# A two-layer hybrid encoder on one Trainium2 core: the recurrent projection is copied to SBUF before its convolution taps

## The chip, the core and the metric

The kernel runs on one core of one Trainium2 chip. The metric is the device time of one execution in microseconds (us). Before the change it is 1476.55 us, the median of three runs (1475.07, 1476.55, 1477.28).

## The reference, cut to what matters

The program computes two residual layers and a final RMS norm over 1024 positions with 1024 channels. The even layer is Fourier mixing beside grouped attention. The change is in the odd layer, a recurrent block of width 2048:

```python
h = rms_norm(x, norm_g)
xr, gate = jnp.split(h @ w_in, 2, axis=-1)            # 2048 recurrent and 2048 gate channels
xp = jnp.pad(xr, ((0, 0), (CONV_LEFT, CONV_WIDTH - 1 - CONV_LEFT), (0, 0)))
xc = conv_b + xp[:, 0:s] * conv_w[0]                  # depthwise, 4 taps at -2, -1, 0, +1
for j in range(1, CONV_WIDTH):
    xc = xc + xp[:, j:j + s] * conv_w[j]
y = (rglru_scan(xc, w_a[0], b_a[0], w_x[0], b_x[0], lam[0], reverse=False)
     + rglru_scan(xc, w_a[1], b_a[1], w_x[1], b_x[1], lam[1], reverse=True))
return x + (y.astype(x.dtype) * jax.nn.silu(gate)) @ w_out
```

`rglru_scan` takes two sigmoid gates of `xc` per direction (block-diagonal matrices of 128x128 over 16 blocks), forms decays from them and runs a linear recurrence along the positions.

## The kernel before, in words

Channels lie on the 128 partitions and positions along the free axis, so a tile `M` is 128x1024 float32 and holds one block of 128 channels. TensorE (PE) multiplies float32 values that are split into a high and a low part: every product is three matmuls (`mm3`, L222 to L224: high by high, high by low, low by high), 128x512 each. A projection of one block is 8 input blocks by 2 halves of the positions by 3, so 48 matmuls. Its result is a PSUM tile `pa` of 128x1024, of which there are three (`A`, L154). A weight arrives by DMA in one of 3 tiles `W`; ACT copies it to a high part `Wh` (L180, the rows CAST Wh<-W), and DVE subtracts that for the low part `Wl` (L181). There are 4 `Wh` and 4 `Wl` tiles, so a CAST Wh waits until PE has read an earlier weight for the last time.

The odd layer (`odd`, L1084) handles its 16 blocks in 16 steps j, which the table `SCHED` (L19) describes. In a step

- **the gate groups**: `gates` (L1112) makes four PSUM tiles, one for each direction and kind of gate, called gate groups 1 to 4 here. Each is 6 matmuls on the split rows of block j, and is emptied by one sigmoid on ACT (L1122);
- **G**: the letter G in `SCHED` is a projection of a gate block, 48 matmuls, emptied by a SiLU on ACT (L1164). In steps 1 to 5 one G lies among the gate groups;
- **P**: the letter P is a recurrent projection, 48 matmuls, followed by `conv` (L1098). In steps 0 to 5 one P lies beside the scans, so step j makes the row of block j+2;
- **the scans**: `scans` (L1125) runs tanh, exp and square root on ACT (L1129 to L1134) and products and two recurrences on DVE (L1128 to L1148).

Later steps hold pieces F of the output projection (`out_part`, L794), whose input is read back from DRAM and split by CAST M<-Q on ACT and a subtraction on DVE. The first eight of those casts stand between steps 5 and 6.

In `conv`, ACT makes the centre tap with the bias straight from PSUM (L1101), and DVE adds the other three taps, also from PSUM (L1105, three instructions), then makes the high part (L1108) and the low part (L1109) that the gate groups multiply. The PSUM tile is free for another product when the third tap has read it.

Instructions are not placed by hand alone. Each engine runs its own queue in order; a scheduling layer (Tile) orders the instructions of each queue from the data they need, from priorities (`self.first(n)`, L188, moves a piece ahead) and from its own estimate of costs. Adding an instruction can therefore move others, on the same engine and on other ones.

Of the kernel before, what the change touches and what calls it, by code (L numbers as in the profile page):

```python
# [137 lines left out]
class Trunk:  # L138
# [945 lines left out]
    def odd(self):  # L1084
        nc, a, par = self.nc, self.a, self.par
# [11 lines left out]

        def conv(j, ps):  # L1098
            with self.first(200):
                xc, xr = self.S(), ps  # L1100
                nc.scalar.activation(xc, ps, AF.Identity, bias=col("cb", j), scale=col("cw", 32 + j))  # L1101
                for tap, o in ((0, -2), (1, -1), (3, 1)):
                    d = slice(max(0, -o), 1024 - max(0, o))
                    s = slice(max(0, o), 1024 + min(0, o))
                    nc.vector.scalar_tensor_tensor(xc[:, d], xr[:, s], col("cw", tap * 16 + j), xc[:, d],  # L1105
                                                   op0=ALU.mult, op1=ALU.add)
                h, low = self.S(F32R), self.S(F32R)
                nc.vector.tensor_copy(h, xc)  # L1108
                nc.vector.tensor_sub(low, xc, h)  # L1109
                return xc, (h, low)  # L1110
# [81 lines left out]
        def item(c):  # L1192
            n = made[c]
            made[c] += 1
            if c == "P":
                return steps(n, lambda ps: rows.__setitem__(n, conv(n, ps)))
            return steps(16 + n, lambda ps: sgs.__setitem__(n, gate_path(n, ps)))
# [8 lines left out]
        for c, (ps, w) in zip(FIRST, start):  # L1206
            self.gemm(ps[:, HALF[1]], w, self.h, HALF[1])
            n = made[c]
            made[c] += 1
            if c == "P":  # L1210
                rows[n] = conv(n, ps)
            else:
                sgs[n] = gate_path(n, ps)
        for _ in items(BEFORE):
            pass
        for j, (kinds, then, chunks) in enumerate(SCHED):
            xc, xhl = rows.pop(j)
# [56 lines left out]
```

## Time and profile before

| | |
|---|---|
| median of the runs | 1476.55 us |
| the profiled execution's own time | 1476.9 us |
| its span, first to last instruction | 1475.1 us |
| PE busy | 1434.8 us (97%) |
| DVE busy | 1177.0 us (80%) |
| ACT busy | 855.7 us (58%) |
| mean granted clock of PE | 0.989 |

All durations below are of this one execution. A row of the profile names the line of the kernel, the engine, the operation and its tiles (`out<-in`, buffer numbers left out). In the timeline the first two numbers are the start and the length in us, and a bracket at the end gives how long the engine had been idle before the instruction and what it waited for. A time there counts from the first instruction of the span. A granted clock of 1.00 is full speed.

### The profile page before, as it was taken

The numbers are of one execution on the slowest core, as the hardware profiler recorded it, in microseconds if no ns is written. First come the engines' busy times: TensorE is split into PE (matmuls) and PEld (weight loads), VectorE is DVE, ScalarE is ACT, GpSimd is POOL, SyncE is SP. The second block draws the span as 40 slices with busy tenths as digits, with TensorE's granted clock in tenths as the row PEclk, the third lists the DMA queues.
The fourth block names the chain that finished last, engine by engine and source line by source line (L and its number), as shares of the span: only waits on it lengthen the run. The fifth ranks groups of instructions, "written<-read, shape, count | busy, mean of one in ns | idle before, by whom it ended". The sixth has DMA issues, their size and how long they took to land.

```text
span 1475.1 us, 17430 instructions
## 1 busy us (share of the span) xinstructions
PE 1434.8 (97%) x6468; PEld 1176.1 (80%) x6468; DVE 1177.0 (80%) x1459; ACT 855.7 (58%) x983; POOL 95.1 (6%) x182
## 2 busy tenths in 40 slices
PE   8999999999998999999999999998999999999997
PEld 6897888888696888788888878777788888887787
DVE  8768979889638787887857768988897989789574
ACT  7635435434326877878734365776658567667143
POOL 0210101000000000000000000000000000001000
PEclk9999999999988999999999999999999999999999
DMA  7733435456655345534456312231413434235552
GB/s 272 268 120 110 172 115 191 171 194 249 243 203 182 129 165 214 179 143 157 144 190 211 127 51 64 72 107 53 147 65 107 129 129 157 79 117 197 168 203 100
DMA packets 79706, 224.67 MB, mean 152 GB/s; under 512 B 9794, under 2 KB 12100, under 8 KB 79620
## 3 DMA queue, kind: packets, MB, share of 16 engines
q1 hardware_dynamic: 60148, 159.40, 33.0%
q0 software_dynamic: 17808, 62.04, 10.7%
q10 hardware_dynamic: 1664, 2.10, 0.4%
q8 instruction: 51, 0.84, 0.2%
q14 instruction: 35, 0.29, 0.1%
HBM read 152.04 MB, written 66.22 MB: 148 GB/s over the span
## 4 chain that ended last, share of the span: by engine, by line
PE 59%; issue 33%; DVE 3%; ACT 2%; POOL 1%; DMA 1%; SPq 0%; POOLq 0%; DVEq 0%; ACTq 0%
PE pa L222 16%; PE pa L223 16%; PE pa L224 15%; PE pb L222 3%; PE pb L223 3%; PE pb L224 2%; PE pb L843 2%; POOL x2d L174 1%; ACT M L180 1%; PE pa L436 1%; PE pb L869 1%; POOL yd L174 1%; DVE M L181 0%; DMA M<-x1d 0%; ACT Wh L180 0%
## 5 line engine op out<-in xcount | busy, mean ns | idle before, releaser
L222 PE MATMUL pa<-M,Wh 128*128 128x512 f32 (+1 forms) x1328 | 514.2, 388 | 17.4 <-ACT M L340 5.5
L223 PE MATMUL pa<-M,Wh 128*128 128x512 f32 (+1 forms) x1328 | 513.4, 387 | 0.2 <-DVE M L181 0.2
L224 PE MATMUL pa<-M,Wl 128*128 128x512 f32 (+1 forms) x1328 | 510.9, 385 | 0.0
L222 PEld LDWEIGHTS pa<-M,Wh 128*128 128x128 f32 x1328 | 250.3, 188 | 74.9 <-ACT M L1122 8.1
L223 PEld LDWEIGHTS pa<-M,Wh 128*128 128x128 f32 x1328 | 250.3, 188 | 52.7 <-DVE M L181 1.8
L224 PEld LDWEIGHTS pa<-M,Wl 128*128 128x128 f32 x1328 | 250.3, 188 | 50.5 <-issue 0.7
L180 ACT CAST Wh<-W 128x1024 fp32r<-128x1024 f32 (+1 forms) x120 | 118.3, 989 | 273.1 <-PE pa L223 190.1
L181 DVE TENSOR_TENSOR Wl<-W,Wh 128x1024 fp32r<-128x1024 f32 (+1 forms) x120 | 137.2, 1147 | 50.4 <-ACT Wh L180 50.3
L180 ACT CAST M<-M 128x1024 fp32r<-128x1024 f32 (+3 forms) x134 | 112.1, 854 | 77.4 <-DVE M L444 35.9
L222 PE MATMUL pa<-M,M 128*128 128x512 f32 (+1 forms) x368 | 144.8, 394 | 10.0 <-DVE M L779 3.4
L181 DVE TENSOR_TENSOR M<-M,M 128x1024 fp32r<-128x1024 f32 (+3 forms) x134 | 128.9, 976 | 28.0 <-ACT M L180 27.2
L223 PE MATMUL pa<-M,M 128*128 128x512 f32 (+1 forms) x368 | 143.2, 389 | 0.2 <-DVE M L181 0.2
L224 PE MATMUL pa<-M,M 128*128 128x512 f32 (+1 forms) x368 | 142.8, 388 | 0.0
L223 PE MATMUL pb<-M,Wh 128*128 128x512 f32 x272 | 106.4, 391 | 2.2 <-DVE M L181 2.2
L222 PE MATMUL pb<-M,Wh 128*128 128x512 f32 x272 | 106.4, 391 | 0.2 <-DVE Q L825 0.2
L224 PE MATMUL pb<-M,Wl 128*128 128x512 f32 x272 | 106.1, 390 | 0.0
L845 DVE TENSOR_REDUCE mx<-pb 128x1 f32<-128x512 f32 x128 | 85.1, 681 | 21.8 <-PE pb L843 21.5
L1122 ACT ACTIVATE M<-pa,par 128x1024 f32<-128x1024 f32 x64 | 70.4, 1116 | 54.2 <-PE pa L224 49.7
L222 PEld LDWEIGHTS pa<-M,M 128*128 128x128 f32 x368 | 71.6, 195 | 26.9 <-ACT M L180 3.3
L904 ACT ACTIVATE M<-pa 128x1024 f32<-128x1024 f32 x64 | 65.7, 1027 | 44.0 <-PE pa L224 43.6
L181 DVE TENSOR_TENSOR M<-Q,M 128x512 fp32r<-128x512 f32 x120 | 77.4, 685 | 11.5 <-ACT M L180 11.4
L180 ACT CAST M<-Q 128x512 fp32r<-128x512 f32 x120 | 69.7, 617 | 28.9 <-DMA Q<-yd 9.7
(221 smaller groups left out, 1926.9 us busy)
## 6 DMA issues: line engine op xcount, KB each, us to landing
W<-wo SPq DMA_DIRECT2D x32, 512.0 KB, 3.7
W<-w SPq DMA_DIRECT2D x32, 512.0 KB, 3.6
W<-wa SPq DMA_DIRECT2D x22, 512.0 KB, 4.5
qd<-M POOLq DMA_DIRECT2D x16, 512.0 KB, 4.0
M<-hd SPq DMA_DIRECT2D x16, 512.0 KB, 4.5
M<-wf SPq DMA_DIRECT2D x16, 512.0 KB, 5.6
M<-qd SPq DMA_DIRECT2D x16, 512.0 KB, 5.7
x1d<-Q POOLq DMA_DIRECT2D x32, 256.0 KB, 2.3
```

Source lines behind the costliest of these rows:

```text
L174: self.nc.gpsimd.dma_start(out=dst, in_=src)
L180: self.nc.scalar.copy(h, src)
L181: self.nc.vector.tensor_sub(l, src, h)
L222: mm(out, w[0], x[0], start=start, stop=False, **k)
L223: mm(out, w[0], x[1], start=False, stop=False, **k)
L224: mm(out, w[1], x[0], start=False, stop=stop, **k)
L436: nc.tensor.matmul(s[:, q], self.onesr, sq.at(q)[l], start=l == 0, stop=l == 1)
L843: nc.tensor.matmul(ps, qh[:, t * 128:t * 128 + 128], self.kh[hd // 4][:, HALF[u]], start=True, stop=True)
L845: nc.vector.reduce_max(mx[:, 2 * t + u:2 * t + u + 1], ps, axis=mybir.AxisListType.X)
L869: nc.tensor.matmul(s, self.onesr, acc[l][:, q], start=l == 0, stop=l == 1)
L904: nc.scalar.activation(e, ps, AF.Exp, scale=SCALE)
L1122: nc.scalar.activation(s, ps, AF.Sigmoid, bias=col("gb", (2 * j + d) * 2 + i))
```

## The change

Two lines of `conv` change. ACT first copies the projection from PSUM to a new tile `xr` in SBUF, and the three taps read that copy. The centre tap still reads PSUM. Everything behind it moves by one line number (L1105 becomes L1106, and so on).

```diff
         def conv(j, ps):
             with self.first(200):
-                xc, xr = self.S(), ps
+                xc, xr = self.S(), self.S()
+                nc.scalar.copy(xr, ps)
                 nc.scalar.activation(xc, ps, AF.Identity, bias=col("cb", j), scale=col("cw", 32 + j))
                 for tap, o in ((0, -2), (1, -1), (3, 1)):
                     d = slice(max(0, -o), 1024 - max(0, o))
                     s = slice(max(0, o), 1024 + min(0, o))
                     nc.vector.scalar_tensor_tensor(xc[:, d], xr[:, s], col("cw", tap * 16 + j), xc[:, d],
                                                    op0=ALU.mult, op1=ALU.add)
```

There are 16 such copies, one for each block, and the scheduling layer orders the queues anew. Three places matter for what follows.

First ACT's queue in step 3, before the change, from the convolution's centre tap on. `pa_7625` is the recurrent projection, `pa_7702`, `pa_7730`, `pa_7751` and `pa_7772` are gate groups 1 to 4, and `Wh_7809` is a weight's high part:

```order
L1101 ACTIVATE M_7684<-pa_7625,par_63 128x1024
L1122 ACT_TABLE_LOAD
L1122 ACTIVATE M_7709<-pa_7702,par_63 128x1024
L1122 ACTIVATE M_7737<-pa_7730,par_63 128x1024
L180 CAST Wh_7809<-W_7711 128x1024
L1122 ACTIVATE M_7758<-pa_7751,par_63 128x1024
L1122 ACTIVATE M_7779<-pa_7772,par_63 128x1024
L1164 ACT_TABLE_LOAD
L1164 ACTIVATE M_7793<-pa_7717 128x1024
L180 CAST Wh_7886<-W_7807 128x1024
```

The same place now, with the copy. `pa_7633` is the projection, `pa_7712`, `pa_7740`, `pa_7761` and `pa_7782` are the gate groups, and `Wh_7819` is the weight that was `Wh_7809`:

```order
L1101 COPY M_7693<-pa_7633 128x1024
L1102 ACTIVATE M_7692<-pa_7633,par_63 128x1024
L180 CAST Wh_7819<-W_7721 128x1024
L1123 ACT_TABLE_LOAD
L1123 ACTIVATE M_7719<-pa_7712,par_63 128x1024
L1123 ACTIVATE M_7747<-pa_7740,par_63 128x1024
L1123 ACTIVATE M_7768<-pa_7761,par_63 128x1024
L180 CAST Wh_7898<-W_7817 128x1024
L1123 ACTIVATE M_7789<-pa_7782,par_63 128x1024
L1165 ACT_TABLE_LOAD
L1165 ACTIVATE M_7803<-pa_7727 128x1024
```

The CAST of the weight stood behind the sigmoids of gate groups 1 and 2 and stands ahead of them now; in both programs it waits for the same instruction of PE, the last but one matmul of step 3's projection G (its last reader is a high-by-low product). The following CAST came up from behind the SiLU to ahead of the fourth sigmoid. Steps 2 and 4 are changed in the same way; in step 5 the CAST (of a 128x512 weight there) stands between the centre tap and the sigmoids in both programs.

Next PE's queue in the same step before the change, around gate group 2 (`pa_7730`), which stands inside the projection G (`pa_7717`) with 40 of its 48 matmuls ahead of it:

```order
L224 MATMUL pa_7717<-M_7017,Wl_7622 128x512
L222 MATMUL pa_7717<-M_7053,Wh_7621 128x512
L222 MATMUL pa_7730<-M_7501,Wh_7525 128x512
L223 MATMUL pa_7730<-M_7502,Wh_7525 128x512
L224 MATMUL pa_7730<-M_7501,Wl_7526 128x512
L222 MATMUL pa_7730<-M_7501,Wh_7525 128x512
L223 MATMUL pa_7730<-M_7502,Wh_7525 128x512
L224 MATMUL pa_7730<-M_7501,Wl_7526 128x512
L223 MATMUL pa_7717<-M_7053,Wh_7621 128x512
```

And now, gate group 2 being `pa_7740` and G `pa_7727`, with 16 of the 48 ahead of it:

```order
L224 MATMUL pa_7727<-M_6785,Wl_7630 128x512
L222 MATMUL pa_7727<-M_6790,Wh_7629 128x512
L222 MATMUL pa_7740<-M_7509,Wh_7533 128x512
L223 MATMUL pa_7740<-M_7510,Wh_7533 128x512
L224 MATMUL pa_7740<-M_7509,Wl_7534 128x512
L222 MATMUL pa_7740<-M_7509,Wh_7533 128x512
L223 MATMUL pa_7740<-M_7510,Wh_7533 128x512
L224 MATMUL pa_7740<-M_7509,Wl_7534 128x512
L223 MATMUL pa_7727<-M_6790,Wh_7629 128x512
```

Gate group 2 moved 24 matmuls towards the start of G. It takes the PSUM tile that the convolution gives back: before, its first matmul waits for the third tap on DVE; now for the centre tap on ACT. Gate groups 3 and 4 still follow the end of G, and each waits for a sigmoid: group 3 for that of group 1, group 4 for that of group 2.

Last, ACT's queue ahead of step 6 before the change, from a centre tap (of `pa_8189`) on: six casts of the output projection's input stand ahead of the weight's CAST and two behind it.

```order
L1101 ACTIVATE M_8248<-pa_8189,par_63 128x1024
L180 CAST M_8262<-Q_8260 128x512
L180 CAST M_8267<-Q_8265 128x512
L180 CAST M_8272<-Q_8270 128x512
L180 CAST M_8277<-Q_8275 128x512
L180 CAST M_8282<-Q_8280 128x512
L180 CAST M_8287<-Q_8285 128x512
L180 CAST Wh_8340<-W_8323 128x1024
L180 CAST M_8292<-Q_8290 128x512
L180 CAST M_8297<-Q_8295 128x512
L1122 ACT_TABLE_LOAD
```

The same place now:

```order
L1101 COPY M_8263<-pa_8203 128x1024
L1102 ACTIVATE M_8262<-pa_8203,par_63 128x1024
L180 CAST Wh_8356<-W_8339 128x1024
L180 CAST M_8278<-Q_8276 128x512
L180 CAST M_8283<-Q_8281 128x512
L180 CAST M_8288<-Q_8286 128x512
L180 CAST M_8293<-Q_8291 128x512
L180 CAST M_8298<-Q_8296 128x512
L180 CAST M_8303<-Q_8301 128x512
L180 CAST M_8308<-Q_8306 128x512
L180 CAST M_8313<-Q_8311 128x512
```

The weight's CAST is ahead of all eight. It waits for PE to reach the end of that step's G in both programs. From step 7 on PE's queue keeps its order, and ACT's gains the copies and moves a few casts.

## The prediction

> **What bounds the kernel now.** I read the page first, then the busy time in stretches of 30 us, PE's waits, and the timeline around those waits.
>
> ```profile
> span 1475.1 us, 17430 instructions
> PE 1434.8 (97%) x6468; PEld 1176.1 (80%) x6468; DVE 1177.0 (80%) x1459; ACT 855.7 (58%) x983; POOL 95.1 (6%) x182
> 1090.00:1120.00 30.00, 30.00 (x134) 24.82 (x133) 25.95 (x23) 15.92 (x16) 1.08 (x2) 1.00 0.29 98
> ```
>
> PE is busy for 97%, and from 1090 to 1330 us, most of the odd layer, it never pauses: 134 matmuls in 30 us, two of them cut by the ends, so 0.226 us each. There, relief of DVE or load on ACT is worth nothing. The change can only act where PE waits, in steps 0 to 6, about 850 to 1062 us. PE's waits there (waiter, waited for, us, times, longest), with one row of the timeline:
>
> ```profile
> PE pa L222 <- DVE M L1105: 4.5, 6, 1.0
> PE pa L222 <- ACT M L1122: 3.7, 2, 2.9
> 865.10 0.47 PE L222 MATMUL pa<-M,Wh 128*128 128x512 f32 x1 [0.24 <-DVE M L1105]
> ```
>
> L1105 is the third tap: PE waits for the PSUM tile that it holds. Step 3 in the timeline:
>
> ```profile
> 947.43 0.39 PE L222 MATMUL pa<-M,Wh 128*128 128x512 f32 x1
> 948.85 0.47 PE L222 MATMUL pa<-M,Wh 128*128 128x512 f32 x1 [1.02 <-DVE M L1105]
> 947.42 1.27 DVE L1105 SCALAR_TENSOR_TENSOR M<-pa,par,M 128x1023 f32<-128x1023 f32 x1
> 940.14 1.19 ACT L1101 ACTIVATE M<-pa,par 128x1024 f32<-128x1024 f32 x1
> 941.34 1.28 ACT L1122 ACT_TABLE_LOAD   x1
> 942.64 1.12 ACT L1122 ACTIVATE M<-pa,par 128x1024 f32<-128x1024 f32 x1
> 950.50 1.12 ACT L1122 ACTIVATE M<-pa,par 128x1024 f32<-128x1024 f32 x1 [6.74 <-PE pa L224]
> 952.08 1.05 ACT L180 CAST Wh<-W 128x1024 fp32r<-128x1024 f32 x1 [0.47 <-PE pa L223]
> ```
>
> The third tap ends at 948.69 and gate group 2 starts 0.16 later. Note the last row: the weight's CAST finds its tile free only at 952.08, when G ends; by then two sigmoids are out of the way. In step 5 it stands ahead of them already:
>
> ```profile
> 997.87 1.18 ACT L1101 ACTIVATE M<-pa,par 128x1024 f32<-128x1024 f32 x1
> 1009.27 0.62 ACT L180 CAST Wh<-W 128x512 fp32r<-128x512 f32 x1 [10.21 <-PE pa L223]
> 1009.91 1.28 ACT L1122 ACT_TABLE_LOAD   x1
> 1011.20 2.12 ACT L1122 ACTIVATE M<-pa,par 128x1024 f32<-128x1024 f32 x2
> 1014.31 1.11 ACT L1122 ACTIVATE M<-pa,par 128x1024 f32<-128x1024 f32 x1 [0.99 <-PE pa L224]
> 1009.07 0.39 PE L224 MATMUL pa<-M,Wl 128*128 128x512 f32 x1
> 1012.37 0.50 PE L222 MATMUL pa<-M,Wh 128*128 128x512 f32 x1 [2.91 <-ACT M L1122]
> ```
>
> ACT stands still for 10.21 us with two finished gate groups behind the CAST. When G ends, PE waits for cast, table load and first sigmoid: 1012.37 - 1009.07 - 0.226 = 3.07 us lost. After its first matmuls PE is slow as well:
>
> ```profile
> 1013.65 0.62 PE L224 MATMUL pa<-M,Wl 128*128 128x512 f32 x1
> 1014.07 0.63 PE L222 MATMUL pa<-M,Wh 128*128 128x512 f32 x1
> ...
> 1017.06 0.40 PE L223 MATMUL pa<-M,Wh 128*128 128x512 f32 x1
> ```
>
> Eight matmuls in 3.41 us instead of 1.81: another 1.6 us.
>
> **What the change does, part by part.** *DVE.* The lines as groups:
>
> ```profile
> L1105 DVE SCALAR_TENSOR_TENSOR M<-pa,par,M 128x1023 f32<-128x1023 f32 x32 | 40.8, 1275 | 0.5
> L1105 DVE SCALAR_TENSOR_TENSOR M<-pa,par,M 128x1022 f32<-128x1022 f32 x16 | 20.4, 1274 | 0.8 <-ACT M L1101 0.8
> L1137 DVE SCALAR_TENSOR_TENSOR M<-M,M 128x1024 f32<-128x1024 f32 x32 | 38.0, 1220 | 32.1 <-ACT M L1131 32.1
> L1164 ACT ACTIVATE M<-pa 128x1024 f32<-128x1024 f32 x16 | 16.4, 1028 | 0.2
> ```
>
> The same operation from SBUF (L1137) takes 1220 ns against 1275: 48 x 0.055 = 2.6 us of DVE. None of it is on the path once PE stops waiting for taps. [...]
>
> *ACT.* 16 copies from PSUM, priced by the SiLU from PSUM without a pointer operand, 1.03 us; bounds are the 1.19 of L1101 and the 0.62 of a 512-wide cast. Sum 16.5 us (10 to 19). No table load comes with them. Behind a copy is queued the rest of a step's ACT work: centre tap, weight cast, sigmoids, and PE waits for the sigmoids. From step 7 PE's saturation covers it; there a copy delays sigmoids by 1 us where PE has tens of matmuls in hand. If that cover failed, ten such copies would cost up to 10 us.
>
> *The waits for taps go.* Of 4.5 us, the 0.24 at 865.10 is followed by waits for the SiLU and the first sigmoid and is given back there. The other five (steps 2 to 6) are 4.26 us by that row; each gap loses 0.17 more than its bracket (947.43 to 948.85 is 1.42, less 0.226 is 1.19), so 5.1 us. What is late next: gate group 2 now follows 16 matmuls of G. In step 3 G began 39 matmuls ahead of 947.43, at 938.62, so it would be reached at 942.24; copy and centre tap end at 940.14 + 0.93 + 1.19 = 942.26 (instructions overlap by 0.1), and PE starts 0.16 later. 0.2 us stays, in four steps 0.8.
>
> *New waits.* In steps 2, 3 and 4 the weight's CAST now stands right behind the centre tap, ahead of the sigmoids, as in step 5, and waits for the end of G. Queued behind it are the table load and the sigmoids of groups 1 and 2; PE needs those tiles for groups 3 and 4. The row for this is step 5's: 3.07, plus 1.05 - 0.62 = 0.43 for the wider cast: 3.5 us. With the slow stretch 1.6 more: 5.1 us a step, 15.3 in three. Bounds: a slow stretch missing, its place is taken by a wait of the next P for the third sigmoid, which starts 1014.31 - 1012.37 = 1.94 after group 3, takes 1.11, and so ends 0.35 after the 12 matmuls of groups 3 and 4 (2.71): 3.85 a step, 11.6 in three. Step 5 keeps its stall.
>
> The other CAST of these steps, which moves from behind the SiLU to ahead of the fourth sigmoid, leaves the ACT work between the first sigmoid and the next copy as long as it was, and I cost it at nothing: what waits for the fourth sigmoid is the next step's group 1, 48 matmuls (10.8 us) further on.
>
> *Tiles and queues.* A copy takes one more of the 37 M tiles, so that ACT's writes wait for users of the tile that are fewer instructions back; by the order these are scans and stores of the step before, more than 10 us old. Cost 0, up to 0.5 a step if a store is late. On SP's queue five loads change places with a neighbour, on POOL's one store does.
>
> ```profile
> W<-w SPq DMA_DIRECT2D x32, 512.0 KB, 3.6
> ```
>
> A weight lands 3.6 us after its issue, and the casts above waited for PE, not for a load: cost 0, and up to 3.6 once if one load came a whole transfer late.
>
> *Step 6.* The weight's CAST moves ahead of the casts M<-Q.
>
> ```profile
> 1031.27 3.21 ACT L180 CAST M<-Q 128x512 fp32r<-128x512 f32 x6
> 1042.16 1.05 ACT L180 CAST Wh<-W 128x1024 fp32r<-128x1024 f32 x1 [7.68 <-PE pa L223]
> 1043.71 3.69 DVE L181 TENSOR_TENSOR M<-Q,M 128x512 fp32r<-128x512 f32 x6
> ```
>
> Six casts were done by 1034.5; now they begin at about 1043.2, the first is out at 1043.8, and DVE, which splits from 1043.71, comes some 0.6 later (0 to 3.2, were all six to be waited for). I take 0.6.
>
> *Sum.* 15.3 + 0.8 + 0.6 - 5.1 = +11.6. Against the profiled execution's own 1476.9 us (its span of 1475.1 and 1.8 around it; the median is 0.35 lower) that is 1488.5 us.
>
> **Is the slow stretch due?** PE's longest pauses, by the rows that end them, and the stretch behind each (columns: PE, PEld, DVE, ACT, POOL busy, granted clock, DMA):
>
> ```profile
> 405.35 0.50 PE L222 MATMUL pa<-M,M 128*128 128x512 f32 x1 [2.89 <-ACT M L180]
> 605.78 0.50 PE L222 MATMUL pa<-M,M 128*128 128x512 f32 x1 [2.48 <-ACT pa L906]
> 1044.45 0.50 PE L223 MATMUL pb<-M,Wh 128*128 128x512 f32 x1 [1.88 <-DVE M L181]
> 405.35:409.75 4.40, 4.18 (x10) 3.15 (x11) 4.17 (x4) 2.75 (x3) 0.00 (x0) 0.61 0.11 14
> 605.78:610.50 4.72, 4.03 (x11) 2.67 (x12) 3.84 (x4) 4.69 (x6) 0.00 (x0) 0.68 0.97 331
> 1044.45:1049.00 4.55, 4.40 (x18) 3.30 (x18) 4.55 (x7) 0.96 (x2) 0.00 (x0) 1.00 0.72 202
> ```
>
> Pauses of 2.48, 2.89 and 2.91 us were followed by a lowered clock, one of 1.88 was not. The new ones would be 3.3, so I expect it each time. [...]
>
> **The rivals.**
>
> *A, the stalls come without slow stretches:* 11.6 + 0.8 + 0.6 - 5.1 = +7.9, 1484.8 us. For it: only three samples. Chance 0.17.
>
> *B, faster: the weight's tile is free when ACT gets there.* Then the CAST costs ACT 1 us and PE nothing, and the five tap waits go: -5.1 + 0.8 = -4.3, 1472.6 us. The point: G's end must come before ACT has finished the centre tap. For it: the waits for taps are the commonest in these steps. Against it: in step 3 the tap ends at 941.3 and the tile comes free at 952.08; in step 5 the CAST waited 10.21 us. Chance 0.04.
>
> *C, no change:* only some steps stall, and the tap waits pay for it; one stall of 3.85 nearly does: within 3 us of 1476.9. Against it: three steps have the same order. Chance 0.03.
>
> *D, worse:* also the casts of step 6 (2.6 more) or a sigmoid behind a copy after step 7 come late: +14 to +16, 1491 to 1493 us. PE shows no wait there now. Chance 0.11.
>
> **How the numbers follow.** The forecast, 1488.5 us, has 0.65. The range 1482.0 to 1492.5 leaves out B, C and the end of D; its lower end is A with 1 us less in each stall. A measurement of this kernel tells 0.2% (3 us) from no change. Faster by more: B, 0.04. Within: 0.03. Slower: 0.93.
>
> **What would show it.** PE's waits for L1105's successor gone; in steps 2, 3 and 4 a gap of 3.5 us between the last matmul of G and group 3, ended by the first sigmoid, with a CAST on ACT ahead that idled some 10 us for PE; granted clock below 0.8 behind each; nothing new after 1100 us but a shift. I am wrong if ACT's CAST there shows no long idle time, or if those gaps are shorter than 2 us.

## The result, and the profile after

The changed kernel takes 1486.79 us, the median of five runs (1485.09 to 1492.86), against 1476.55 us before, the median of five runs (1475.07 to 1478.83). The ratio over all runs is 1.0078 (95% interval 1.0062 to 1.0094; the two medians alone give 1.0069). It is slower by some 10 us; the forecast was 1488.5. One of the five runs, 1492.86, lies just above the forecast's range.

The head of the page:

```profile
span 1484.9 us, 17457 instructions
...
PE 1435.3 (97%) x6468; PEld 1176.7 (79%) x6468; DVE 1177.5 (79%) x1459; ACT 869.9 (59%) x999; POOL 95.0 (6%) x182
```

ACT is busy 14.2 us longer, DVE not a microsecond less. PE's waits in steps 0 to 6 (850 to 1072 us; waiter, waited for, us, times, longest):

```profile
PE pa L222 <- ACT M L1123: 13.7, 5, 3.3
PE pb L223 <- DVE M L181: 2.4, 1, 2.4
PE pb L222 <- ACT M L180: 1.4, 1, 1.4
```

The waits for the third tap (now L1106) have left the list. Waits for a sigmoid (L1123) have come in: before they were 3.7 us in two pieces.

ACT's queue in step 3, in the timeline (start, length, instruction, idle time ahead and what ended it):

```profile
943.35 0.99 ACT L1101 COPY M<-pa 128x1024 f32<-128x1024 f32 x1
944.25 1.21 ACT L1102 ACTIVATE M<-pa,par 128x1024 f32<-128x1024 f32 x1
954.26 1.04 ACT L180 CAST Wh<-W 128x1024 fp32r<-128x1024 f32 x1 [8.81 <-PE pa L223]
955.33 1.28 ACT L1123 ACT_TABLE_LOAD   x1
956.62 2.12 ACT L1123 ACTIVATE M<-pa,par 128x1024 f32<-128x1024 f32 x2
```

The CAST stands directly behind the centre tap. ACT does nothing for 8.81 us, until PE has read the weight for the last time, and the sigmoids of two gate groups that PE finished long before stand behind it. PE in steps 3 and 4:

```profile
954.07 0.39 PE L224 MATMUL pa<-M,Wl 128*128 128x512 f32 x1
957.79 0.50 PE L222 MATMUL pa<-M,Wh 128*128 128x512 f32 x1 [3.34 <-ACT M L1123]
958.12 0.39 PE L223 MATMUL pa<-M,Wh 128*128 128x512 f32 x1
...
985.07 0.39 PE L224 MATMUL pa<-M,Wl 128*128 128x512 f32 x1
988.80 0.50 PE L222 MATMUL pa<-M,Wh 128*128 128x512 f32 x1 [3.34 <-ACT M L1123]
...
990.46 0.63 PE L222 MATMUL pa<-M,Wh 128*128 128x512 f32 x1
...
993.02 0.61 PE L222 MATMUL pa<-M,Wh 128*128 128x512 f32 x1
993.45 0.42 PE L223 MATMUL pa<-M,Wh 128*128 128x512 f32 x1
```

Each step loses 957.79 - 954.07 - 0.226 = 3.49 us ahead of group 3; step 2 loses the same. Step 4 has a stretch at half pace behind it (0.43 us a matmul up to 993.45), and so has step 2. Step 3 has none: its second matmul starts 0.33 us after the first, and then they go at 0.23.

Two landmarks give the stage's length: the start of gate group 4 in step 0, and the first L223 of the output projection's first piece in step 6 (before, that row is the one at 1044.45). Before:

```profile
869.23 0.50 PE L222 MATMUL pa<-M,Wh 128*128 128x512 f32 x1 [0.76 <-ACT M L1122]
...
1376.83 0.50 PE L222 MATMUL pa<-M,Wh 128*128 128x512 f32 x1 [0.78 <-ACT M L180]
```

After, with the wait ahead of the second landmark and a late one near the end:

```profile
868.17 0.50 PE L222 MATMUL pa<-M,Wh 128*128 128x512 f32 x1 [0.76 <-ACT M L1123]
...
1051.45 0.50 PE L222 MATMUL pb<-M,Wh 128*128 128x512 f32 x1 [1.43 <-ACT M L180]
1054.38 0.50 PE L223 MATMUL pb<-M,Wh 128*128 128x512 f32 x1 [2.43 <-DVE M L181]
...
1386.58 0.50 PE L222 MATMUL pa<-M,Wh 128*128 128x512 f32 x1 [0.79 <-ACT M L180]
```

The stage took 1044.45 - 869.23 = 175.2 us before and 1054.38 - 868.17 = 186.2 after: 11.0 us more. This execution of the changed kernel came into the stage 1.06 us earlier than that of before, so it left it 9.93 us later, and at the late row, some 330 us on, it is 1386.58 - 1376.83 = 9.75 us behind. All of the loss lies in steps 0 to 6.

### The profile page after: what moved, and what is told of

The parts are those of the page before. It is cut to its first block, busy times and chain, and to the rows that moved or that the text cites. A ratio compares the mean times of both kernels' runs of the same rounds, so it can differ in the third digit from the quotient of the medians.

```text
span 1484.9 us, 17457 instructions
## 1 busy us (share of the span) xinstructions
PE 1435.3 (97%) x6468; PEld 1176.7 (79%) x6468; DVE 1177.5 (79%) x1459; ACT 869.9 (59%) x999; POOL 95.0 (6%) x182
## 4 chain that ended last, share of the span: by engine, by line
PE 87%; DVE 5%; ACT 4%; DMA 2%; issue 2%; SPq 0%; DVEq 0%; ACTq 0%
PE pa L222 24%; PE pa L223 24%; PE pa L224 24%; PE pb L223 4%; PE pb L222 4%; PE pb L224 4%; PE pb L843 2%; ACT M L180 1%; DVE M L181 1%; DMA M<-x1d 1%; PE pa L436 1%; ACT L1123 1%; DVE M L1146 1%; PE pb L869 1%; ACT Wh L180 1%
## 5 line engine op out<-in xcount | busy, mean ns | idle before, releaser
L222 PE MATMUL pa<-M,Wh 128*128 128x512 f32 (+1 forms) x1328 | 515.5, 389 | 22.9 <-ACT M L1123 14.7
L223 PE MATMUL pa<-M,Wh 128*128 128x512 f32 (+1 forms) x1328 | 514.6, 388 | 0.4 <-DVE M L181 0.4
L222 PEld LDWEIGHTS pa<-M,Wh 128*128 128x128 f32 x1328 | 251.1, 189 | 80.1 <-ACT M L1123 18.6
L223 PEld LDWEIGHTS pa<-M,Wh 128*128 128x128 f32 x1328 | 251.2, 189 | 53.4 <-DVE M L181 2.0
L181 DVE TENSOR_TENSOR Wl<-W,Wh 128x1024 fp32r<-128x1024 f32 (+1 forms) x120 | 137.2, 1147 | 51.7 <-ACT Wh L180 51.6
L222 PE MATMUL pa<-M,M 128*128 128x512 f32 (+1 forms) x368 | 143.3, 390 | 10.8 <-DVE M L779 3.5
L181 DVE TENSOR_TENSOR M<-M,M 128x1024 fp32r<-128x1024 f32 (+3 forms) x134 | 129.0, 977 | 28.0 <-ACT M L180 27.2
L223 PE MATMUL pa<-M,M 128*128 128x512 f32 (+1 forms) x368 | 141.9, 386 | 0.2 <-DVE M L181 0.2
L223 PE MATMUL pb<-M,Wh 128*128 128x512 f32 x272 | 107.1, 394 | 2.4 <-DVE M L181 2.4
L222 PE MATMUL pb<-M,Wh 128*128 128x512 f32 x272 | 107.2, 394 | 1.4 <-ACT M L180 1.4
L222 PEld LDWEIGHTS pa<-M,M 128*128 128x128 f32 x368 | 70.5, 192 | 27.6 <-ACT M L180 3.3
L181 DVE TENSOR_TENSOR M<-Q,M 128x512 fp32r<-128x512 f32 x120 | 77.7, 684 | 10.5 <-ACT M L180 10.4
L1123 ACT ACTIVATE M<-pa,par 128x1024 f32<-128x1024 f32 x64 | 70.0, 1115 | 25.6 <-PE pa L224 20.1
```

The costliest lines, as they stand in the source:

```text
L181: self.nc.vector.tensor_sub(l, src, h)
L222: mm(out, w[0], x[0], start=start, stop=False, **k)
L223: mm(out, w[0], x[1], start=False, stop=False, **k)
L1123: nc.scalar.activation(s, ps, AF.Sigmoid, bias=col("gb", (2 * j + d) * 2 + i))
```

## The experiments

Two theories were to be told apart. *Queue theory*: what costs is a CAST that waits for the end of G at a place in ACT's queue where sigmoids stand behind it; the copies cost next to nothing, and the relief of the tap waits is a gain of a few us. *The copies' own price*: 16 more microseconds on ACT, and taps that begin later, cost the time, whatever the order.

| kernel | median, us | ratio to before, 95% interval | stage, us |
|---|---|---|---|
| before | 1476.55 | | 175.2 |
| changed | 1486.79 | 1.0078, 1.0062 to 1.0094 | 186.2 |
| e1: copy, CAST later | 1469.44 | 0.9964, 0.9951 to 0.9977 | 169.5 |
| e2: no copy, CAST later | 1473.22 | 0.9983, 0.9973 to 0.9992 | 172.4 |
| e3: copy, read by nobody | 1488.59 | 1.0098, 1.0078 to 1.0118 | |
| e4: copy made twice | 1490.58 | 1.0098, 1.0081 to 1.0116 | 188.9 |
| e5: copy of 8 columns, unread | 1475.58 | 0.9999, 0.9990 to 1.0009 | 175.2 |
| e6: e1 with output piece later | 1469.62 | 0.9960, 0.9946 to 0.9975 | 168.4 |
| e9: copy, fifth weight tile | 1482.70 | 1.0050, 1.0035 to 1.0065 | 168.7 |
| e10: no copy, fifth weight tile | 1485.93 | 1.0075, 1.0060 to 1.0090 | 171.8 |

Each experiment's ratio is to runs of the kernel before that were made together with the experiment (their medians lie between 1474.4 and 1475.9 us), so it is not the quotient of two medians of this table. The stage lengths are differences of the same two landmarks in the one trace of each kernel (e3 has no wait that marks the first one). The second landmark lies ahead of the half clock that followed it in e1 (2.2 us, as e6's expectation has it); the stage leaves that out.

### e1 and e2: the CAST held back, with and without the copy

The split of the next step's gate weights, which comes up while G begins, is kept until the second sigmoid has been issued, and pinned behind it on ACT. The split after it, the one that waited for G, then comes later too. The same edit is made in both kernels:

```diff
         if n == len(self.ready) and n >= 0:
+            if self.hold:
+                self.held.append(n)
+                return
...
+    def release(self):
+        self.hold = False
+        for n in self.held:
+            c = self.order[n]
+            with self.first(100):
+                h, l = (self.S(F32R, (128, c[3] - c[2]), t) for t in ("Wh", "Wl"))
+                self.tc.keep_in_program_order(self.nc.scalar.copy(h, self.raw[n]))
+                self.nc.vector.tensor_sub(l, self.raw[n], h)
+            self.ready.append((h, l))
+        self.held = []
...
                         nc.scalar.activation(s, ps, AF.Sigmoid, bias=col("gb", (2 * j + d) * 2 + i))
+                    n = 2 * d + i
+                    if n == 1:
+                        self.release()
+                    self.hold = n == 0
                     yield s
```

Line numbers grow by 16 (L222 becomes L238, L1123 L1139; the held CAST is L222, the others L181).

> The changed kernel, with one weight's CAST of each step held back in the program until the second sigmoid has been issued, so that in steps 2 to 6 no weight's CAST stands between the centre tap and the sigmoids any more; copy and taps are as in the changed kernel. Queue theory (the loss is the CAST that waits for the end of G ahead of the sigmoids): PE's gaps of 3.5, 3.5, 3.5 and 3.1 us ahead of gate group 3 in steps 2 to 5 go, with the slow stretches behind three of them (4.9 us), and most of step 6's extra 2.3 us; 1486.8 - 13.6 - 4.9 = 1468, some 8 us below the kernel before (1466 to 1473). Rival, the copies' own price (16 more microseconds on ScalarE, and taps that start later): the order doesn't matter, 1484 to 1488.

> The kernel before (no copy), with the CAST held back in the same way. Queue theory: only step 5 had the CAST ahead of its sigmoids, so its 3.1 us gap and the slow stretch of 1.6 us go, and the five waits for taps stay (5.1 us in all): 1476.6 - 4.7 = 1472, with the waits for L1105's successor still in PE's list. If the copy's relief of the tap waits is real, this stays 3 to 4 us above the copy kernel with the same order. Rival: no difference from the kernel before, 1476.6.

ACT's queue of e1 in step 3:

```profile
940.16 1.21 ACT L1118 ACTIVATE M<-pa,par 128x1024 f32<-128x1024 f32 x1
941.38 1.28 ACT L1139 ACT_TABLE_LOAD   x1
942.67 2.12 ACT L1139 ACTIVATE M<-pa,par 128x1024 f32<-128x1024 f32 x2
944.69 0.62 ACT L222 CAST Wh<-W 128x512 fp32r<-128x512 f32 x1
950.81 1.05 ACT L181 CAST Wh<-W 128x1024 fp32r<-128x1024 f32 x1 [5.51 <-PE pa L239]
```

The CAST waits as it did, 5.51 us, but both sigmoids are out ahead of it. PE's waits of e1, 850 to 1072 us:

```profile
PE pb L239 <- DVE M L182: 4.6, 1, 4.6
PE pa L238 <- ACT M L1139: 0.8, 1, 0.8
```

And of e2:

```profile
PE pa L238 <- DVE M L1121: 5.3, 7, 0.9
PE pb L239 <- DVE M L182: 3.0, 2, 2.6
```

In e1 the stalls and the tap waits are both gone; in e2 the tap waits (L1121) remain. With the CAST held back the copy is a gain: 169.5 against 172.4 us in the stage, 1469.4 against 1473.2 in the medians. Both totals are close to what was expected (1468 and 1472). The same 16 copies, 16 us of ACT, that stood in a kernel 10 us slower now stand in one 5 to 6 us faster than before (ratio 0.9964). The copies' own price falls as the cause. One part of e1's expectation failed: step 6 gave nothing back, and PE waits there for the low parts of the output projection's input (L182) for 4.6 us.

### e3: the copy made, and read by nobody

```diff
-                    nc.vector.scalar_tensor_tensor(xc[:, d], xr[:, s], col("cw", tap * 16 + j), xc[:, d],
+                    nc.vector.scalar_tensor_tensor(xc[:, d], ps[:, s], col("cw", tap * 16 + j), xc[:, d],
```

> The changed kernel with the copy still made but read by nobody: the three taps read the PSUM tile as in the kernel before. The ScalarE order of steps 2 to 6 is that of the changed kernel. Queue theory: the stalls ahead of group 3 stay (3.5 us each, 3.1 in step 5), and the waits for the third tap come back in five steps, each about 0.9 us longer than in the kernel before because the taps start behind copy and centre tap (1.0 to 2.1 us each where 0.2 to 0.4 is left in the changed kernel): 1486.8 + 5 x 1.7 = 1495 (1490 to 1498). If reading the copy is what costs, on VectorE or through the tile's life, it falls back towards 1477.

```profile
PE pa L222 <- ACT M L1123: 10.5, 4, 3.3
PE pa L222 <- DVE M L1106: 6.9, 7, 2.1
```

The stalls stay without anybody reading the copy: it is its presence in the queue that brings them. The size was expected too high (1488.6 for 1495). The waits for taps came back with 0.8 to 1.0 us each in steps 2 to 6, not 1.0 to 2.1 (the longest in the list, 2.1 us, is in step 0), because the scheduling layer answered the later taps: in the program's order of steps 2, 3, 4 and 6 group 2 now stands behind 45 matmuls of G (40 to 43 in the kernel before, 16 or 17 in the changed kernel). In step 5 it even stands behind all 48, and there the wait for the sigmoid shrank to 0.52 us.

### e4: the copy made twice

```diff
                 nc.scalar.copy(xr, ps)
+                nc.scalar.copy(xr, ps)
```

> The changed kernel with each copy made twice in a row, 16 more copies of 0.99 us, order otherwise as in the changed kernel. Queue theory: the centre tap ends 0.9 us later, PE's wait ahead of gate group 2 grows from 0.2-0.4 to 1.1-1.3 us in steps 2 to 6, and nothing is added from step 7 on: +4.5 us, 1491 (1488 to 1494). Rival, the copies' own price: as much again as the change cost, +10 us, 1497, or +16 if each lies on the path.

```profile
PE pa L222 <- ACT M L1124: 13.7, 5, 3.3
PE pb L223 <- DVE M L181: 3.4, 1, 3.4
```

The time was as expected (1490.6 for 1491), the reason not. No wait ahead of group 2 appears; in the program's order it had moved from behind 16 matmuls of G to behind 20 (in step 5 from 17 to 22), and 4 x 0.226 is the 0.9 us of the second copy. The stage is 2.7 us longer: 1.0 is the wait for L181 in step 6 (3.4 for 2.4); most of the rest I put down to half clock: the mean granted clock of this execution was 0.984, for 0.989 in the changed kernel's. Of 16 us more on ACT, 1 us can be found as a wait. Its runs (1487.0 to 1492.2) overlap with those of the changed kernel.

### e5: a copy of 8 columns

```diff
-                nc.scalar.copy(xr, ps)
+                nc.scalar.copy(xr[:, :8], ps[:, :8])
```

The taps read PSUM here, as in e3.

> The kernel before, with a copy of only 8 of the 1024 columns of each projection ahead of the centre tap, read by nobody; the taps read the PSUM tile. 16 more ScalarE instructions and a tile more in use for each step, but the centre tap ends hardly later, and the order keeps the sigmoids ahead of the weight's CAST in steps 2 to 4, as in the kernel before. Queue theory: no stalls of 3.5 us, time as before, 1476 (1474 to 1479). Rival, the additional instruction and its tile are what cost: 1480 to 1488.

```profile
PE pa L222 <- DVE M L1106: 4.5, 6, 1.0
PE pa L222 <- ACT M L1123: 3.7, 2, 2.9
PE pb L223 <- DVE M L181: 1.9, 1, 1.9
```

But for half a microsecond these are the waits of the kernel before, and so is the time (ratio 0.9999). The additional instruction and its tile cost nothing that can be measured. Between e5 and e3 only the copy's length differs, so it is the length that brings the other order. That the scheduling layer puts the CAST first because it reckons with a centre tap that ends a microsecond later is the likely reason; no run shows its reckoning.

### e6: an output piece one place later

```diff
-SCHED = "/P/0 G/P/0 G/P/0 G/P/0 G/P/0 G/P/2 G//2 G/PPG/1 /G/0 P//5 PP/G/5 /G/3 P/GF/1 P/G/3 P/G/2 G//6"
+SCHED = "/P/0 G/P/0 G/P/0 G/P/0 G/P/0 G/P/1 G//3 G/PPG/1 /G/0 P//5 PP/G/5 /G/3 P/GF/1 P/G/3 P/G/2 G//6"
```

> The copy kernel with the CAST held back (1469.4), and one of the two output pieces planned behind step 5 moved behind step 6. In that kernel PE still lost 4.75 us in step 6, waiting for VectorE's low parts of the first output piece's inputs, and 2.2 us of half clock after it. With the piece one place later those inputs are split while PE does the next projections: both go, 1469.4 - 7 = 1462.5 (1461 to 1467). If the wait only moves to another place, 1467 to 1471.

No gain over e1: 1469.6 for 1469.4. The total is in the range that was given for a wait that only moves, but the wait did not move: in the program's order the first matmuls of the output projection still stand right behind step 6's G, as in e1, and PE still waits there, 3.4 us after 4.6 (the first row; below it DVE ahead of that wait):

```profile
PE pb L239 <- DVE M L182: 3.4, 1, 3.4
...
1029.99 1.22 DVE L1169 TENSOR_TENSOR M<-M,M 128x1024 f32<-128x1024 f32 x1
1031.12 1.22 DVE L1126 TENSOR_TENSOR M<-M,M 128x1024 fp32r<-128x1024 f32 x1
1032.26 3.70 DVE L182 TENSOR_TENSOR M<-Q,M 128x512 fp32r<-128x512 f32 x6
```

DVE works without a pause, and the low parts that PE waits for (L182) stand in its queue behind taps, scans and the row's own low part. What is late next is DVE's queue, and the edit of the table doesn't change that.

### e7 and e8: taps with a constant

```diff
-                    nc.vector.scalar_tensor_tensor(xc[:, d], xr[:, s], col("cw", tap * 16 + j), xc[:, d],
+                    nc.vector.scalar_tensor_tensor(xc[:, d], xr[:, s], 0.25, xc[:, d],
```

> The kernel before with the constant 0.25 in place of the tap weight's column in the three taps (the convolution is a different one); the taps read PSUM. My prediction took the 1275 ns of a tap against the 1220 ns of L1137 for the price of PSUM; the changed kernel's taps take 1275 from SBUF as well. Theory: the scalar that is read from a tile costs the 55 ns: 1220 ns a tap here. Rival, the shape costs it (1023 or 1022 elements at an odd offset): 1275 stays. Rival, PSUM costs it after all and the changed kernel hides that: 1275 here, 1220 in the run beside it.

> The changed kernel with the constant 0.25 in place of the tap weight's column in the three taps (the convolution is a different one); the taps read the copy in SBUF. Theory, the scalar from a tile costs 55 ns: 1220 ns a tap. Rival, the shape: 1275. The time falls by 48 x 0.055 = 2.6 us of VectorE at most, which isn't on the path: as the changed kernel, 1485 to 1492.

The changed kernel's taps from SBUF with the weight's column, as groups (count, total us, mean ns):

```profile
L1106 DVE SCALAR_TENSOR_TENSOR M<-M,par,M 128x1023 f32<-128x1023 f32 x32 | 40.8, 1275 | 0.5
```

With the constant, from PSUM (the kernel e7):

```profile
L1105 DVE SCALAR_TENSOR_TENSOR M<-pa,M 128x1023 f32<-128x1023 f32 x32 | 38.9, 1216 | 0.5
```

With the constant, from SBUF (e8):

```profile
L1106 DVE SCALAR_TENSOR_TENSOR M<-M,M 128x1023 f32<-128x1023 f32 x32 | 38.9, 1217 | 0.5
```

PSUM or SBUF makes no difference: 1216 and 1217 ns with the constant, 1275 and 1275 with the column. The scalar that is read from a tile makes one: 59 ns. One run each: 1477.1 us for e7, 1491.2 for e8; the first is in the range of the runs of the kernel before, the second in that of the changed kernel.

### e9 and e10: a fifth tile for split weights

```diff
-        self.bufs = {"M": 37, "Q": 6, "W": 3, "Wh": 4, "Wl": 4}
+        self.bufs = {"M": 35, "Q": 6, "W": 3, "Wh": 5, "Wl": 5}
```

> The changed kernel with five tiles for split weights in place of four (Wh and Wl; M falls from 37 to 35 to make room). The CAST still stands right behind the centre tap in steps 2 to 5, ahead of the sigmoids, but its tile has been free for long, so it doesn't wait for the end of G; in step 6 it still waits. Queue theory (the wait costs, not the place nor the copy): the gaps of 3.5, 3.5, 3.5 and 3.1 us and their slow stretches go, 1486.8 - 13.6 - 4.9 = 1468 (1466 to 1473), though ScalarE does the same work in the same order. Rival, ScalarE's load of copy, tap and cast ahead of the sigmoids: the gaps stay, 1484 to 1488. Two M tiles fewer could cost a few us in both of this pair.

> The kernel before with five tiles for split weights and 35 M tiles, the control of the run with the copy. Queue theory: step 5's gap of 3.1 us and its slow stretch go, 1476.6 - 4.7 = 1472 (1470 to 1475), and the waits for the third tap stay, so that it is some 3 to 4 us above the same with the copy. Rival: the tiles themselves change the time of both by the same amount, and the copy stays 10 us behind.

ACT of e9 in step 3, and PE at a place in a later step:

```profile
937.16 1.00 ACT L1101 COPY M<-pa 128x1024 f32<-128x1024 f32 x1
938.05 1.21 ACT L1102 ACTIVATE M<-pa,par 128x1024 f32<-128x1024 f32 x1
939.16 1.04 ACT L180 CAST Wh<-W 128x1024 fp32r<-128x1024 f32 x1
...
941.51 2.12 ACT L1123 ACTIVATE M<-pa,par 128x1024 f32<-128x1024 f32 x2
...
1217.63 0.80 PE L222 MATMUL pa<-M,Wh 128*128 128x512 f32 x1 [6.02 <-ACT M L1165]
```

The order is the changed kernel's, copy, centre tap, CAST, sigmoids, but the CAST has no idle time in front of it, and PE stalls in none of steps 2 to 5. The wait for the end of G has passed to the next CAST, behind the two sigmoids (5.36 us ahead of the one at 948.99). The stage is short, 168.7 us. So the wait ahead of the sigmoids costs, not the place of the CAST and not ACT's load. The totals were expected wrong, 1482.7 for 1468 and 1485.9 for 1472: both kernels have new waits behind the stage, the longest of them 6.0 us at 1217 us for a SiLU. Whether two M tiles fewer or the new order brings these was not tried. The pair's difference, 3.2 us in favour of the copy, is that of e1 and e2 again.

## Why the prediction was right, step by step

| term | forecast, us | measured, us |
|---|---|---|
| three stalls ahead of group 3 | 3 x 3.5 = 10.5 | 3.49 + 3.49 + 3.50 = 10.5 |
| half-clock stretches behind them | 3 x 1.6 = 4.8 | 1.7 + 0 + 1.6 = 3.3 |
| tap waits that go | -5.1 | -5.1 |
| what stays ahead of group 2 | 0.8 | 0.4 |
| step 6 | 0.6 | 2.3 |
| sum | +11.6 | +11.4; +11.0 by the landmarks |

*The bound and the saturated rest* were right: behind step 6 nothing changes but the shift. The copy took 0.99 us, for 1.03 in the forecast.

*The stalls* were right in place, length and cause. The CAST in steps 2, 3 and 4 has 8.8 us of idle time ahead of it, and e1, e3 and e9 show each link: with the sigmoids ahead, no stall; with an unread copy, the stall; with a free tile, no stall in the same order.

*The tap waits* went. 0.4 us is an estimate: in three of the five steps the first matmuls of group 2 come late, by 0.1 to 0.2 us each, beside what one missing record of a matmul explains. The copy's worth for itself, forecast at -5.1 + 0.8 = -4.3 us in rival B, is -2.9 and -3.1 us in the stage in the two pairs (e1 and e2, e9 and e10); part of it is given back in step 6.

*The half-clock stretches* were right in two of three. The step that failed is "the new ones would be 3.3, so I expect it each time": a pause's length alone did not decide it: behind step 2's pause of 3.49 us there was a stretch, behind step 3's, as long, there was none (last section). Rival A, which wanted none, got one of three. A stretch behind step 6's pause, some 1.7 us up to 1058.36, was not in the sum at all. It lies behind the second landmark, where two waits of the kernel before (0.5 and 0.4 us, at 1049 and 1051) are gone, and the 9.75 us at the late row show no more loss from it.

*Step 6* was mis-sized, 2.3 us for 0.6, with the wrong reason. I let the six casts come late and DVE with them. In fact PE first waits 1.43 us for the cast and then 2.43 for a low part, and DVE had work up to it:

```profile
1051.38 1.21 DVE L1149 TENSOR_TENSOR M<-M,M 128x1024 f32<-128x1024 f32 x1
1052.51 1.21 DVE L1110 TENSOR_TENSOR M<-M,M 128x1024 fp32r<-128x1024 f32 x1
1053.65 3.69 DVE L181 TENSOR_TENSOR M<-Q,M 128x512 fp32r<-128x512 f32 x6
```

Its queue sets 1053.65, not the casts. e1 confirms it: there the six casts ran right behind the centre tap, and PE still waited 4.59 us for the low parts.

*DVE's 2.6 us* failed, without effect on the sum: DVE is busy 1177.5 us after 1177.0. I had put the 55 ns between a tap and L1137 down to PSUM; e7 and e8 show that it is the scalar from a tile. So copying to SBUF first gave DVE nothing in this kernel. What it gave, in e1 over e2, is the earlier release of the PSUM tile: the tap waits in e2's list, 5.3 us, are gone in e1's.

*The cover behind step 7* held: PE's idle time behind 1072 us is 3.6 us in the changed kernel and 4.2 in e4, with 4.0 in the kernel before.

The forecast of 1488.5 us stands 1.7 above the measured 1486.8. 1.06 of that is the earlier entry of this execution into the stage; the rest are the terms above, of which a stretch too many and a step 6 too cheap offset each other. That the total came so close is in part luck; the stalls, the largest term, are not.

## What to carry to other kernels

An instruction that waits in an in-order queue costs what stands behind it, not what it does itself (here a CAST of 1.04 us waited 8.81, and PE lost 3.49 us to the sigmoids behind it): before pricing an added instruction, look where a scheduler puts its neighbours, and which of them waits for another engine. When a change that ought to help slows a kernel, try it once more with the order held: here the copy was worth some 3 us, and the reordering that came with it cost 14 (10.5 of stalls, 3.3 of half clock). A resource that is freed earlier helps until the next engine's queue is late, which here was DVE's, a few microseconds on: in e1 PE waited 4.6 us for it.

## What the runs showed of the hardware

**Half clock came in stretches of 3.41 us, and not behind every long pause.** In the changed kernel's trace the granted clock was 0.50 in four stretches of steps 2 to 6 (busy time of PE, PEld, DVE, ACT and POOL, then the granted clock):

```profile
925.22:928.63 3.41, 3.41 (x8) 2.73 (x9) 3.41 (x4) 1.40 (x2) 0.50 (x1) 0.50 0.20 43
...
990.07:993.49 3.42, 3.42 (x10) 2.65 (x9) 2.47 (x3) 1.78 (x2) 0.53 (x1) 0.50 0.50 163
...
1020.79:1024.21 3.42, 3.36 (x8) 2.69 (x9) 3.42 (x4) 1.41 (x3) 0.30 (x1) 0.50 0.25 35
...
1054.93:1058.34 3.41, 3.41 (x9) 2.60 (x8) 3.41 (x5) 0.62 (x1) 0.00 (x0) 0.50 0.78 239
```

The distances from one end to the next, 64.86, 30.72 and 34.13 us, are 19, 9 and 10 times 3.413 us to within 0.02 us. Here is what stood ahead of step 4's stretch, and, in steps of the same length counted from 928.63, around the pause of step 3:

```profile
952.53:955.94 3.41, 1.92 (x9) 1.26 (x7) 3.41 (x4) 1.66 (x2) 0.00 (x0) 1.00 0.00 0
955.94:959.35 3.41, 1.56 (x7) 1.30 (x8) 3.41 (x4) 2.79 (x3) 0.00 (x0) 1.00 0.00 0
...
986.66:990.07 3.41, 1.27 (x6) 1.05 (x7) 3.41 (x4) 3.08 (x3) 0.00 (x0) 1.00 0.00 0
```

PE stood for 2.14 us of the last of these, up to 988.80, and the next one is slow. In step 3 the boundary at 955.94 cuts the pause of 3.49 us (954.30 to 957.79) into 1.64 and 1.85, and no stretch follows. From 620 to 1455 us the traces of the two kernels have five half-clock stretches, these four and one from 1013.65 to 1017.06 in the kernel before. In the 3.41 us ahead of each, one pause took 2.13 us or more (a pause counts from 0.226 us after the start of the last matmul); of the other 3.41 us at full clock, counted in the same steps, none held a longer one than 1.96 us (1040.96 to 1044.37 before). That the place of a pause in these steps decides is my estimate from the two traces; no run varied it alone. It does not hold ahead of 620 us, where the changed kernel has half clock behind 3.4 us without a pause of PE:

```profile
426.87:430.29 3.42, 3.42 (x34) 3.42 (x32) 0.00 (x0) 0.00 (x0) 0.00 (x0) 1.00 1.02 363
430.29:433.70 3.41, 3.41 (x19) 3.41 (x19) 0.89 (x3) 1.91 (x4) 0.00 (x0) 0.50 0.76 276
```

The same kernel got different clocks from run to run: the mean granted clock lay between 0.982 and 0.989 in the five runs of the changed kernel. e8 differs from it by a constant, and its matmuls have the same order up to the second landmark; its mean granted clock was 0.986, for 0.989 in the changed kernel's trace, and its stage is 190.8 us long, for 186.2.

**With the scalar read from a tile, a `scalar_tensor_tensor` of DVE took 59 ns longer** (1275 ns in the changed kernel, 1216 with the constant in e7), and a source in PSUM made no difference (1216 ns in e7, 1217 from SBUF in e8), in 128x1023 float32 with two tensor inputs.
